# First mixer: the low halves of 38 weight blocks on VectorE instead of GpSimd

## The chip, the cores and the metric

The kernel runs on one core of a Trainium2 chip. The metric is the device time of one execution in microseconds (us); lower is better. A core has engines that run side by side, each through its own list of instructions in order: TensorE (PE in the profile, with the loading of its weights as PEld) multiplies matrices, VectorE (DVE), ScalarE (ACT) and GpSimd (POOL) work element by element, and SyncE (SP) issues most of the loads from HBM.

## The reference

A network of two blocks on 256 tokens of width 1024, in float32. What matters here is the first block's mixer:

```
mod = silu(c) @ w_ada + b_ada                       # 6 x 1024 values: shift, scale, gate, twice
hn  = modulate(rmsnorm(x, norm1_g), shift1, scale1)
qa, ka, va, qi, ki, wi, qb, kb, vb, ga, gb = split(hn @ w_in)
ya  = dsa_attention(...)             # scores by qi, ki, wi choose 64 keys a token; softmax over them
yb  = stick_breaking_attention(qb, kb, vb)
merged = sigmoid(ga) * (ya @ w_proj_a) + sigmoid(gb) * (yb @ w_proj_b)
x   = x + gate1 * (merged @ w_out)
f   = peer_ffn(modulate(rmsnorm(x, norm2_g), shift2, scale2), ...)   # begins with h @ w_q
```

Behind it come the expert layer (`peer_ffn`, whose queries are the "query blocks" below), and the second block with its own mixer, a cross attention and a feed-forward part.

## The kernel before

**Products in two halves.** TensorE gets every operand as a high half (the value rounded to the type of fp32r) and a low half (the value minus the high half), and a product is three matmuls: high by high, high by low and low by high (`mm3`, lines 129 to 131). `weights` (line 90 loads, lines 98 and 100 compute) fetches one block of 128 x 1024 weights, 512 KB, into `wraw`, makes the high half `wh` on ScalarE (L98), and the low half `wl` on VectorE or GpSimd (L100), by the argument `eng`: "v" or "g". There are four buffers for `wraw` and three each for `wh` and `wl`; a `wraw` buffer comes free when both halves are made, a pair of halves when TensorE has read them. A projection block is 24 matmuls on one such weight block. In the lists below a number behind a name tells the buffers of one block from those of another (`wh_1500`, `wl_820`).

**The first mixer.** The first 13 weight blocks (with an order of their own, `ORDER`) end at about 70 us. Then the string `PLAN` sets the order in which steps are written: i and j score the tokens and take the top 64 by eight rounds of max and replace (`index`, L507 to L516, on VectorE), a, v, q and k are projections, s the steps of the first attention (L521 to L645, copies of its transposed weights `pT` at L676, products at L693), 0 to 3 the four pairs of heads of the stick-breaking attention (`stick`: products L708, L731, L745; VectorE at L720 to L739), g one of 16 gate blocks, and r one of 24 adaLN rows. An adaLN row (`ada_one`) is a load of 512 KB and a multiply with a sum over 128 x 1024 elements on VectorE (L266); its two buffers, `lateqx` and `latekx`, are filled in turn. Then the outputs of both attentions are projected (`w_proj`), multiplied by the gates (L568 to L572), split (`mg`, L118 and L119) and projected by `w_out`. The keys and values of the second block's memory are prepared in between (L125, L188, L195, `hm`). At about 290 us the second norm follows (`adaln`, L278 to L281), and the query blocks of the expert layer, the first two of which run together as the norm's columns come.

**What sets the order.** A scheduler of the framework puts each engine's instructions in an order by a model of its own, within the dependences; each engine then goes through its list strictly. Loads of this part are issued in the order of the code (`load`, `in_turn`). So a load that waits for its buffer holds all that follow, and an instruction that waits holds all that stand behind it on its engine.

In the kernel before, the 32 blocks of `w_in` that follow the first 13, the first of each pair of `w_proj` blocks (4), and the first two query blocks have `eng="g"`, 38 in all. 46 blocks of the expert layer, between about 340 and 480 us, have it as well.

Of the kernel before, what the change touches and what calls it, by code (L numbers as in the profile page):

```python
# [31 lines left out]
FIRST = 2  # L32
# [38 lines left out]
class Net:  # L71
# [212 lines left out]
    def first_mixer(self):  # L284
        nc, tc, ap = self.nc, self.tc, self.ap
        with ExitStack() as es:
# [26 lines left out]
            ps = self.ps([128, T], "sm")  # L313
# [25 lines left out]
            hn = self.hi_lo("hn0")  # L339
# [42 lines left out]
            for e in ORDER:  # L382
                if e == "a":
                    k = known
# [20 lines left out]
                with tc.issue_after(norm_exp.ins), tc.issue_after(self.last_rsqrt.ins):  # L405
                    w = self.weights(ap["w_in"][len(first) if e == "w" else 9 + c], next(nlow),
                                     spare.pop() if e == "w" else None)
# [18 lines left out]
            ps = banks[4][:, 0]  # L426
# [10 lines left out]
            def behind():  # L437
                if todo:
                    j = todo.pop(0)
                    self.ada_one(A, j, late[j % 2])  # L440

            def blocks(j0, outs, scale=1.0):
                for j, t in enumerate(outs):
                    ps = self.fm_block(self.weights(ap["w_in"][j0 + j], "g"), hn)
                    yield
                    nc.scalar.activation(t, ps, AF.Copy, scale=scale)  # L446
                    yield

            def chunks(j0, t):
                pss = [self.ps([128, 512], "acc") for _ in range(2)]  # L450
                for k in range(KT):
                    if k % 2 == 0:
                        w = self.weights(ap["w_in"][j0 + k // 2], "g")
                    o = k % 2 * 512
                    for tb in range(2):
                        ts = slice(tb * 128, tb * 128 + 128)
                        self.mm3(pss[tb], (hn[0][:, k, ts], hn[1][:, k, ts]), (w[0][:, o:o + 512], w[1][:, o:o + 512]),
                                 k == 0, k == KT - 1)
                    if k % 2:
                        yield  # L460
                        if k == KT - 1:
                            for tb in range(2):
                                nc.scalar.activation(t[:, tb], pss[tb], AF.Copy)
                        yield

            wi = P.tile([128, 2, 8], FT, name="wi")
            ps = self.ps([128, 2, 8], "sm")
# [4 lines left out]
            with tc.issue_after(qi_last.ins):  # L472
# [4 lines left out]
                ps = self.ps([128, 384], "sm")  # L477
# [8 lines left out]
                for tb in range(2):  # L486
# [3 lines left out]
                                                   ap=[[8 * 384 - 1, 128], [384, 8], [1, n]]))  # L490
# [34 lines left out]
            def attention():  # L525
                pT = None
                for pT in self.probs(P, qa, ka, 8, True, bias, dsa, fine=True):
# [6 lines left out]
            ya, yb = [[P.tile([128, 4, T], FR, name=f"y{c}{i}") for i in range(2)] for c in "ab"]  # L534
            sg = [P.tile([128, 8, T], FT, name=nm) for nm in ("sga", "sgb")]
            gates = blocks(29, [t[:, j] for t in sg for j in range(8)])
            steps = {"i": index(0), "j": index(1), "a": blocks(13, [qa[:, j] for j in range(4)]),
                     "q": blocks(17, [qk[:, 0, j] for j in range(4)], 0.125),
                     "k": blocks(21, [qk[:, 1, j] for j in range(4)]), "v": chunks(25, vb), "s": attention(), "g": gates}
            for hp in range(4):  # L540
                steps[str(hp)] = self.stick(W, hp, qk[:, 0], qk[:, 1], vb, yb)
# [17 lines left out]

            mg = self.hi_lo("mg")  # L560
            for j2 in range(4):
                wa = self.weights(ap["w_proj"][2 * j2], "g")
                wb = self.weights(ap["w_proj"][2 * j2 + 1])
                for i in range(2):
                    j = 2 * j2 + i
                    pa = self.fm_block(wa, ya, 4, i * 512, self.ps([128, T], "acc"))
                    m = W.tile([128, T], FT, name="m")
                    nc.vector.tensor_mul(m, pa, sg[0][:, j])  # L568
                    pb = self.fm_block(wb, yb, 4, i * 512, self.ps([128, T], "acc"))
                    m2 = W.tile([128, T], FT, name="m2")  # L570
                    nc.vector.tensor_mul(m2, pb, sg[1][:, j])
                    nc.vector.tensor_add(m, m, m2)  # L572
                    self.split(mg[0][:, j], mg[1][:, j], m)
                    behind()
# [9 lines left out]
            for j in range(8):  # L584
                ps = self.fm_block(self.weights(ap["w_out"][j]), mg)
# [166 lines left out]
    def peer(self):  # L752
        nc, tc, ap = self.nc, self.tc, self.ap
        hn = self.hn2
        P = self.ctx.enter_context(tc.tile_pool(name="p1", bufs=1))
        with ExitStack() as es:
# [8 lines left out]
            q = carve("q", 16, T)  # L765
            sk = carve("sk", 16, 128)
            nc.scalar.dma_start(sk, ap["sub_keys"])
            ws = [self.weights(ap["peer_wq"][j], "g") for j in range(FIRST)]
            pss = [self.ps([128, T], "acc") for _ in range(FIRST)]
            for k in range(KT):  # L770
                o = slice(k * 128, k * 128 + 128)
# [2 lines left out]
            for j in range(16):  # L774
                ps = pss[j] if j < FIRST else self.fm_block(self.weights(ap["peer_wq"][j]), hn)
# [155 lines left out]
            for e in range(126):  # L931
# [15 lines left out]
                if e >= 96 and e % 2 == 0 and e < 112:  # L947
                    k = (e - 96) // 2
                    nc.vector.tensor_scalar(xg[:, k], x[:, k], g23[:, 0, k:k + 1], None, op0=OP.mult)
                c = v_coef(e)  # L950
                w = self.weights(ap["peer_v"][e])
# [566 lines left out]
```

## Time and profile before

| what | value |
|---|---|
| time, median of 3 runs | 1478.95 us (1477.77 to 1479.18) |
| the profiled execution | 1477.79 us, span of its instructions 1476.0 us |
| mean granted clock of TensorE | 0.982 |
| TensorE busy | 1389.3 us (94% of the span) |
| VectorE busy | 1103.3 us (75%) |
| ScalarE busy | 755.4 us (51%) |
| GpSimd busy | 247.5 us (17%) |
| moved by DMA | 269.52 MB, 183 GB/s in the mean |

The profile is of one execution, so what is read from it stands against 1477.79 us, 1.16 us under the median. Busy shares are means over parts of the program with different limits; TensorE is the fullest engine over the whole, and VectorE in some of its parts. The granted clock is TensorE's share of its full rate: 1.0 is 2.4 GHz, 0.5 is 1.2 GHz. In rows on a wait, what stands behind the arrow is the instruction that ended it.

### The profile page before, as it was taken

The numbers are of one execution on the slowest core, as the hardware profiler recorded it, in microseconds if no ns is written. First come the engines' busy times: TensorE is split into PE (matmuls) and PEld (weight loads), VectorE is DVE, ScalarE is ACT, GpSimd is POOL, SyncE is SP. The second block draws the span as 40 slices with busy tenths as digits, with TensorE's granted clock in tenths as the row PEclk, the third lists the DMA queues.
The fourth block names the chain that finished last, engine by engine and source line by source line (L and its number), as shares of the span: only waits on it lengthen the run. The fifth ranks groups of instructions, "written<-read, shape, count | busy, mean of one in ns | idle before, by whom it ended". The sixth has DMA issues, their size and how long they took to land. (4 is left out here: it accounts for less than half of the span.)

```text
span 1476.0 us, 28894 instructions
## 1 busy us (share of the span) xinstructions
PE 1389.3 (94%) x11584; PEld 1334.0 (90%) x11584; DVE 1103.3 (75%) x2044; ACT 755.4 (51%) x1358; POOL 247.5 (17%) x102
## 2 busy tenths in 40 slices
PE   4987988989998999999999999999999999899997
PEld 3876878989998999999999999999999889789996
DVE  7677868646999988999966555666557786777776
ACT  4544635445445555555454444444445465655555
POOL 3356532105999000000000000000000000000001
PEclk9999989999999999999999999999999999999998
DMA  7765854654555555555566665776564445256562
GB/s 281 250 199 201 280 175 161 205 193 156 174 184 166 173 154 168 158 159 157 165 194 216 202 190 190 228 233 215 186 187 157 128 134 171 72 173 196 189 191 95
DMA packets 76235, 269.52 MB, mean 183 GB/s; under 512 B 8970, under 2 KB 11202, under 8 KB 75460
## 3 DMA queue, kind: packets, MB, share of 16 engines
q1 hardware_dynamic: 71426, 257.99, 54.5%
q10 hardware_dynamic: 4674, 9.69, 1.9%
q8 instruction: 90, 1.47, 0.4%
q14 instruction: 45, 0.37, 0.1%
HBM read 265.01 MB, written 4.21 MB: 182 GB/s over the span
## 5 line engine op out<-in xcount | busy, mean ns | idle before, releaser
L98 ACT ACTIVATE wh<-wraw 128x1024 fp32r<-128x1024 f32 x431 | 456.2, 1060 | 521.1 <-PE ps_acc L130 243.1
L100 DVE TENSOR_TENSOR wl<-wraw,wh 128x1024 fp32r<-128x1024 f32 x346 | 423.9, 1227 | 245.3 <-ACT wh L98 243.9
L129 PE MATMUL ps_acc<-c,wh 128*128 128x256 f32 x1024 | 286.5, 280 | 0.0
L131 PE MATMUL ps_acc<-c,wl 128*128 128x256 f32 x1024 | 286.4, 280 | 0.0
L130 PE MATMUL ps_acc<-c,wh 128*128 128x256 f32 x1024 | 286.4, 280 | 0.0
L100 POOL TENSOR_TENSOR wl<-wraw,wh 128x1024 fp32r<-128x1024 f32 x85 | 228.1, 2700 | 194.0 <-ACT wh L98 151.2
L131 PE MATMUL ps_acc<-hn,wl 128*128 128x256 f32 x696 | 192.7, 277 | 6.2 <-POOL wl L100 6.2
L131 PE MATMUL ps_mm<-hn,wl 128*128 128x256 f32 x680 | 191.3, 282 | 6.4 <-POOL wl L100 6.4
L129 PE MATMUL ps_mm<-hn,wh 128*128 128x256 f32 x680 | 194.7, 286 | 2.0 <-ACT sga L446 1.0
L129 PE MATMUL ps_acc<-hn,wh 128*128 128x256 f32 x696 | 193.9, 279 | 0.0
L129 PEld LDWEIGHTS ps_acc<-c,wh 128*128 128x128 f32 x1024 | 192.5, 188 | 0.1
L130 PE MATMUL ps_acc<-hn,wh 128*128 128x256 f32 x696 | 192.4, 277 | 0.1
L130 PEld LDWEIGHTS ps_acc<-c,wh 128*128 128x128 f32 x1024 | 192.5, 188 | 0.0
L131 PEld LDWEIGHTS ps_acc<-c,wl 128*128 128x128 f32 x1024 | 192.5, 188 | 0.0
L130 PE MATMUL ps_mm<-hn,wh 128*128 128x256 f32 x680 | 191.5, 282 | 0.0
L1404 POOL TENSOR_TENSOR big<-big 128x512 f32<-128x512 f32 x4 | 5.0, 1264 | 982.0 <-DVE big L1401 982.0
L131 PEld LDWEIGHTS ps_mm<-hn,wl 128*128 128x128 f32 x680 | 130.8, 192 | 7.2 <-POOL wl L100 7.2
L131 PEld LDWEIGHTS ps_acc<-hn,wl 128*128 128x128 f32 x696 | 130.7, 188 | 7.2 <-POOL wl L100 7.2
L129 PEld LDWEIGHTS ps_mm<-hn,wh 128*128 128x128 f32 x680 | 131.3, 193 | 4.6 <-issue 1.3
L130 PEld LDWEIGHTS ps_mm<-hn,wh 128*128 128x128 f32 x680 | 131.0, 193 | 0.2
L130 PEld LDWEIGHTS ps_acc<-hn,wh 128*128 128x128 f32 x696 | 130.8, 188 | 0.3 <-DVE hn L281 0.3
L129 PEld LDWEIGHTS ps_acc<-hn,wh 128*128 128x128 f32 x696 | 130.6, 188 | 0.1
(484 smaller groups left out, 2821.9 us busy)
## 6 DMA issues: line engine op xcount, KB each, us to landing
wraw<-in_peer_u_dram SPq DMA_DIRECT2D x128, 512.0 KB, 3.9
wraw<-in_peer_v_dram SPq DMA_DIRECT2D x128, 512.0 KB, 4.2
wraw<-in_w_in_dram SPq DMA_DIRECT2D x70, 512.0 KB, 4.4
wraw<-in_ffn_up_dram SPq DMA_DIRECT2D x44, 512.0 KB, 3.6
wraw<-in_ffn_down_dram SPq DMA_DIRECT2D x22, 512.0 KB, 3.6
ada<-in_w_ada_dram SPq DMA_DIRECT2D x16, 512.0 KB, 6.5
wraw<-in_w_out_dram SPq DMA_DIRECT2D x16, 512.0 KB, 4.5
wraw<-in_peer_wq_dram SPq DMA_DIRECT2D x16, 512.0 KB, 3.6
```

The costliest lines, as they stand in the source:

```text
L98: nc.scalar.activation(h, raw, AF.Copy)
L100: (nc.vector if eng == "v" else nc.gpsimd).tensor_tensor(l, raw, h.bitcast(FT), op=OP.subtract)
L129: mm(out, a[0], b[0], start=first, stop=False, **kw)
L130: mm(out, a[0], b[1], start=False, stop=False, **kw)
L131: self.last_mm = mm(out, a[1], b[0], start=False, stop=last, **kw)
L1404: nc.gpsimd.tensor_tensor(xf[:, tb, cs], xt[:, tb, cs], fg[:, cs], op=OP.mult)
```

## The change

Four calls of `weights` lose their `"g"`, so that the low halves of those 38 blocks are computed by VectorE. The arithmetic is the same.

```
             def blocks(j0, outs, scale=1.0):
                 for j, t in enumerate(outs):
-                    ps = self.fm_block(self.weights(ap["w_in"][j0 + j], "g"), hn)
+                    ps = self.fm_block(self.weights(ap["w_in"][j0 + j]), hn)
...
                     if k % 2 == 0:
-                        w = self.weights(ap["w_in"][j0 + k // 2], "g")
+                        w = self.weights(ap["w_in"][j0 + k // 2])
...
             for j2 in range(4):
-                wa = self.weights(ap["w_proj"][2 * j2], "g")
+                wa = self.weights(ap["w_proj"][2 * j2])
...
-            ws = [self.weights(ap["peer_wq"][j], "g") for j in range(FIRST)]
+            ws = [self.weights(ap["peer_wq"][j]) for j in range(FIRST)]
```

The scheduler also sets other instructions in another order. Three places follow. The first is ScalarE, near the end of the first attention: `wh_1444` and `wh_1500` are high halves of two gate blocks, `sga` and `qk` results of projections, `pT` the transposed weights of the attention's last heads, `ya` its output. Before:

```order
L98 ACTIVATE wh_1444<-wraw_1442 128x1024
L446 ACTIVATE sga_643<-ps_mm_1293 128x256
L98 ACTIVATE wh_1500<-wraw_1498 128x1024
L446 ACTIVATE qk_637<-ps_mm_1328 128x256
L676 ACTIVATE pT0_881<-ps_sm_1354 128x2x128
L676 ACTIVATE pT1_882<-ps_sm_1354 128x2x128
L118 ACTIVATE ya0_639<-ps_sm_1361 128x256
```

and in the changed kernel, on the same engine from the same high half:

```order
L98 ACTIVATE wh_1444<-wraw_1442 128x1024
L446 ACTIVATE qk_637<-ps_mm_1328 128x256
L676 ACTIVATE pT0_881<-ps_sm_1354 128x2x128
L676 ACTIVATE pT1_882<-ps_sm_1354 128x2x128
L1229 DMA mem_1990<-in_mem_dram 128x2048
L118 ACTIVATE ya0_639<-ps_sm_1361 128x256
L118 ACTIVATE ya0_639<-ps_sm_1368 128x256
L98 ACTIVATE wh_1500<-wraw_1498 128x1024
```

The high half `wh_1500` stood ahead of the two copies of `pT`; now it stands behind them and behind two outputs of the attention.

The second place is VectorE ahead of L726 of the third pair of stick-breaking heads (`l1_1704`), on which TensorE's product L731 waits. `junk_1872`, `junk_1875` and `junk_1956` are adaLN rows. Before:

```order
L266 SCALAR_TENSOR_TENSOR junk_1872,mod_82<-lateqx_1121,cond_103 128x1024
L739 TENSOR_TENSOR lb_1484<-lb_1484,upper_98 128x2x2x128
L266 SCALAR_TENSOR_TENSOR junk_1875,mod_82<-latekx_1122,cond_103 128x1024
L270 TENSOR_TENSOR mod_82<-mod_82,b_ada_81 128x8
L582 SCALAR_TENSOR_TENSOR gs_83<-mod_82,vecs_80 128x8
L119 TENSOR_TENSOR yb1_642<-ps_sm_1714,yb0_641 128x256
L720 SCALAR_TENSOR_TENSOR lb_1703<-ps_acc_1696,az_1702 128x384
L720 SCALAR_TENSOR_TENSOR lb_1703<-ps_acc_1699,az_1702 128x384
L721 TENSOR_TENSOR l1_1704<-lb_1703,ps_acc_1696 128x384
L721 TENSOR_TENSOR l1_1704<-lb_1703,ps_acc_1699 128x384
L266 SCALAR_TENSOR_TENSOR junk_1956,mod_82<-lateqx_1121,cond_103 128x1024
L726 TENSOR_TENSOR l1_1704<-l1_1704,upper_98 128x2x2x128
```

and in the changed kernel, the rows that end with the same L726:

```order
L100 TENSOR_TENSOR wl_1784<-wraw_1781,wh_1783 128x1024
L739 TENSOR_TENSOR lb_1484<-lb_1484,upper_98 128x2x2x128
L266 SCALAR_TENSOR_TENSOR junk_1824,mod_82<-lateqx_1121,cond_103 128x1024
L270 TENSOR_TENSOR mod_82<-mod_82,b_ada_81 128x8
L266 SCALAR_TENSOR_TENSOR junk_1827,mod_82<-latekx_1122,cond_103 128x1024
L119 TENSOR_TENSOR yb1_642<-ps_sm_1714,yb0_641 128x256
L720 SCALAR_TENSOR_TENSOR lb_1703<-ps_acc_1696,az_1702 128x384
L720 SCALAR_TENSOR_TENSOR lb_1703<-ps_acc_1699,az_1702 128x384
L721 TENSOR_TENSOR l1_1704<-lb_1703,ps_acc_1696 128x384
L721 TENSOR_TENSOR l1_1704<-lb_1703,ps_acc_1699 128x384
L100 TENSOR_TENSOR wl_1832<-wraw_1829,wh_1831 128x1024
L726 TENSOR_TENSOR l1_1704<-l1_1704,upper_98 128x2x2x128
```

The rows 1872, 1875 and 1956 have moved behind L726, and low halves have come in among the others.

The third place is VectorE at the end of the first top-k (`acc0`, L515) and the beginning of the second (`acc1`). `wl_820`, `wl_852`, `wl_924` and `wl_942` are low halves of the projections a, a, v and q. Before:

```order
L507 SCALAR_TENSOR_TENSOR acc1_635<-rel_696,wi_613,acc1_635 128x256
L514 MATCH_REPLACE acc0_634<-m8_667,acc0_634 128x128
L515 TENSOR_SCALAR acc0_634<-acc0_634 128x128
L516 TENSOR_TENSOR acc0_634<-acc0_634,cm_94 128x128
L507 SCALAR_TENSOR_TENSOR acc1_635<-rel_706,wi_613,acc1_635 128x256 x2
L507 SCALAR_TENSOR_TENSOR acc1_635<-rel_710,wi_613,acc1_635 128x256 x2
L513 MAX m8_714<-acc1_635 128x8
L514 MATCH_REPLACE acc1_635<-m8_714,acc1_635 128x256
```

and in the changed kernel:

```order
L507 SCALAR_TENSOR_TENSOR acc1_635<-rel_696,wi_613,acc1_635 128x256
L515 TENSOR_SCALAR acc0_634<-acc0_634 128x128
L100 TENSOR_TENSOR wl_820<-wraw_817,wh_819 128x1024
L516 TENSOR_TENSOR acc0_634<-acc0_634,cm_94 128x128
L507 SCALAR_TENSOR_TENSOR acc1_635<-rel_706,wi_613,acc1_635 128x256 x2
L507 SCALAR_TENSOR_TENSOR acc1_635<-rel_710,wi_613,acc1_635 128x256 x2
L100 TENSOR_TENSOR wl_852<-wraw_849,wh_851 128x1024
L513 MAX m8_714<-acc1_635 128x8
L100 TENSOR_TENSOR wl_924<-wraw_921,wh_923 128x1024
L514 MATCH_REPLACE acc1_635<-m8_714,acc1_635 128x256
L100 TENSOR_TENSOR wl_942<-wraw_939,wh_941 128x1024
```

Four low halves stand among the rounds of the top-k now.

## Rows read from the trace of the kernel before

**Rows 1.** Busy time of the engines by stretch, in us, with granted clock and DMA.

```profile
core 0: us, PE busy (x) PEld busy (x) DVE busy (x) ACT busy (x) POOL busy (x), PEclk, DMA share, GB/s
66.00:113.00 47.00, 42.07 (x286) 36.71 (x285) 31.23 (x88) 23.02 (x47) 26.08 (x11) 0.96 0.60 193
113.00:196.00 83.00, 64.94 (x509) 57.91 (x509) 71.64 (x98) 44.27 (x93) 44.89 (x18) 0.93 0.67 238
196.00:256.00 60.00, 54.15 (x404) 52.04 (x403) 40.81 (x72) 29.34 (x45) 17.16 (x7) 0.90 0.49 164
...
66.00:300.00 234.00, 203.31 (x1550) 188.11 (x1549) 174.77 (x310) 117.31 (x218) 92.88 (x37) 0.94 0.60 202
```

**Rows 2.** TensorE's waits, 66 to 300 us: total us, times, longest.

```profile
PE ps_sm L693 <- ACT pT L676: 7.0, 1, 7.0
PE ps_sm L731 <- DVE l L726: 5.3, 1, 5.3
PE ps_mm L131 <- POOL wl L100: 3.8, 2, 2.2
PE ps_acc L131 <- POOL wl L100: 2.9, 2, 1.5
...
PE ps_acc L131 <- DVE wl L100: 2.7, 2, 2.4
PE ps_sm L188 <- DVE yb L119: 1.8, 1, 1.8
```

**Rows 3.** Groups, 66 to 300 us: busy us, mean ns; idle before, its releasers.

```profile
L100 POOL TENSOR_TENSOR wl<-wraw,wh 128x1024 fp32r<-128x1024 f32 x37 | 92.9, 2521 | 137.6 <-ACT wh L98 95.0 <-DVE diag L218 41.6 <-PE ps_sm L469 1.1
...
L100 DVE TENSOR_TENSOR wl<-wraw,wh 128x1024 fp32r<-128x1024 f32 x17 | 20.8, 1222 | 2.6 <-ACT wh L98 1.7
```

**Rows 4.** Groups of VectorE, 113 to 196 us.

```profile
L266 DVE SCALAR_TENSOR_TENSOR junk<-lateqx,cond 128x1024 f32<-128x1024 f32 x9 | 17.8, 1982 | 0.8 <-DMA lateqx<-in_w_ada_dram 0.8
L266 DVE SCALAR_TENSOR_TENSOR junk<-latekx,cond 128x1024 f32<-128x1024 f32 x8 | 16.5, 2064 | 1.0 <-DMA latekx<-in_w_ada_dram 1.0
L645 DVE TENSOR_SCALAR bias<-bias,st 128x256 f32<-128x256 f32 x8 | 6.2, 816 | 0.0
...
L739 DVE TENSOR_TENSOR lb<-lb,upper 128x512 f32<-128x512 f32 x2 | 3.6, 1776 | 0.9 <-ACT lb L738 0.9
L635 DVE TENSOR_SCALAR st<-st 128x2 f32<-128x2 f32 x4 | 2.8, 701 | 0.0
```

**Rows 5.** Line 266, the whole span: ns shortest/median/longest.

```profile
L266 DVE SCALAR_TENSOR_TENSOR junk<-lateqx,cond x12: 1207/1225/3422, 126.8 to 234.3; 128x1024 f32<-128x1024 f32 x12
```

**Rows 6.** Timeline, 129 to 148 us: start, us, instruction, idle before.

```profile
129.71 11.09 POOL L100 TENSOR_TENSOR wl<-wraw,wh 128x1024 fp32r<-128x1024 f32 x4 [3.42 <-ACT wh L98]
...
135.17 3.42 DVE L266 SCALAR_TENSOR_TENSOR junk<-lateqx,cond 128x1024 f32<-128x1024 f32 x1
...
139.05 0.86 SPq L90 DMA_DIRECT2D wraw<-in_w_in_dram  x2
...
144.87 1.06 ACT L98 ACTIVATE wh<-wraw 128x1024 fp32r<-128x1024 f32 x1 [7.75 <-DMA wraw<-in_w_in_dram]
...
147.06 0.42 DVE L119 TENSOR_TENSOR ya<-ps_sm,ya 128x256 fp32r<-128x256 f32 x1 [3.61 <-ACT ya L118]
```

**Rows 7.** Timeline of VectorE, 120 to 123 us.

```profile
120.27 0.15 DVE L635 TENSOR_SCALAR st<-st 128x2 f32<-128x2 f32 x1
...
122.27 0.60 DVE L645 TENSOR_SCALAR bias<-bias,st 128x256 f32<-128x256 f32 x2
```

**Rows 8.** Timeline of VectorE, 189 to 194 us.

```profile
189.92 2.74 DVE L266 SCALAR_TENSOR_TENSOR junk<-lateqx,cond 128x1024 f32<-128x1024 f32 x1
...
192.59 0.68 DVE L726 TENSOR_TENSOR l<-l,upper 128x512 f32<-128x512 f32 x1
```

**Rows 9.** Timeline of VectorE, 234 to 238 us.

```profile
234.27 3.42 DVE L266 SCALAR_TENSOR_TENSOR junk<-lateqx,cond 128x1024 f32<-128x1024 f32 x1
```

**Rows 10.** Timeline of TensorE and VectorE, 82 to 84 us.

```profile
82.58 0.28 PE L129 MATMUL ps_mm<-hn,wh 128*128 128x256 f32 x1
...
83.54 0.23 DVE L515 TENSOR_SCALAR acc<-acc 128x128 f32<-128x128 f32 x1
```

## The prediction, made before the changed kernel ran

> **What bounds the kernel now.** I read five views, from wide to narrow. The first is the busy time of each engine by stretch [rows 1]. All but one of the moved subtractions run between 66 and 300 us, 37 of the 38 (the other stands just ahead of it). In these 234.0 us TensorE works 203.3 us and stands 30.7 us, and the granted clock is 0.94, which means it spent part of the stretch at 1.2 GHz instead of 2.4. Everything that the change can win lies in these two numbers; a reader should see that the rest of the span can only shift. The second view is TensorE's waits in that stretch [rows 2]. The six rows carry 23.5 of the 30.7 us. Only 6.7 us (3.8 and 2.9) name the moved operation itself. The two longest single waits, 7.0 us for a copy on ScalarE and 5.3 us for a VectorE multiply, don't name it, and the question is whether they hang on it all the same.
>
> The third view, the groups by line [rows 3], says that they do. One low half takes 2.52 us on GpSimd and 1.22 us on VectorE. But VectorE pays for GpSimd's work too: the adaLN rows of L266 take between 1.21 and 3.42 us [rows 5], and their mean in the stretch 113 to 196, by their two buffers, is 1.98 and 2.06 us [rows 4]. The long ones lie beside GpSimd: while four subtractions run there one behind the other from 129.7 to 140.8, a row of L266 takes 3.42 us [rows 6]. So an operation with two operands in SBUF stands on VectorE until GpSimd has finished its own. The stretch 113 to 196 is the tight one: VectorE is busy 71.6 of 83.0 us, more than TensorE's 64.9 [rows 1].
>
> **The change, stage by stage.** It removes 38 operations of about 2.5 us from GpSimd and adds 38 of 1.22 us to VectorE, 46 us in all. Nothing is added to ScalarE or the load queue. The order of the instructions changes on VectorE, ScalarE and (from 230 us on) TensorE.
>
> *113 to 196 us: 18 operations.* VectorE's work first. Added: 18 x 1.22 = 22.0 us. Given back: the 17 rows of L266 take 17.8 + 16.5 = 34.3 us and would take 17 x 1.21 = 20.6, so 13.7; L645 takes 6.2 us for eight that take 0.60 a pair undisturbed, so 3.8; L739 takes 3.6 for two, where the same shape takes 0.68 in L726, so 2.2; L635 takes 2.8 for four of 0.15, so 2.2 [rows 4, 5, 7, 8]. Together 21.9 us. VectorE's work stays as it is: 71.6 - 21.9 + 22.0 = 71.7 us. What changes is when its results come.
>
> The 7.0 us wait: TensorE stands at 139.8 for the copy of pT, and that copy stands on ScalarE behind the high half wh_1500, which waits 7.75 us for its weights to land [rows 6]. Their load was issued at 139.05, since the queue's load before it refills the buffer of the stretched L266 row, which ended at 138.5. In the new order wh_1500 stands behind both pT copies, and the row of L266 isn't stretched. This wait goes. What is late next is the load itself, which the block two further on needs. The 5.3 us wait for L726: in the old order three rows of L266 (1872, 1875 and 1956) stand ahead of it, the last of them 2.74 us long [rows 8]; in the new one all three stand behind it, and one low half (wl_1832) comes ahead. This wait goes too, unless VectorE as a whole is late.
>
> So the stage is bounded by VectorE from both sides. If its 11.4 us of idle time (83.0 - 71.6) stay, nothing is won. If all of it goes and the three deferred rows (3 x 1.21 = 3.6 us) fall into later idle time as well, 15 us are won; TensorE's 64.9 us would allow 18. I take 7: 3.6 us of VectorE's idle time lie inside the 7.0 us wait (it waits 3.61 us for ScalarE, until 147.1 [rows 6]), and 3.6 are the deferred rows.
>
> *196 to 256 us: 7 operations.* VectorE is busy 40.8 of 60.0 us and has room [rows 1]. The waits here are 1.4 us of the 2.9 for GpSimd, 2.4 us of the 2.7 for a low half that already is on VectorE, and 1.8 us for yb [rows 2]. The 2.4 us one stands behind an L266 row of 3.42 us [rows 9], stretched by GpSimd, and goes with it. Yb stands behind an L266 row as well, and goes. Of the 1.4 us I let half stay, since the low half stands on VectorE behind a product of the same block (L568). That is 0.7 + 2.4 + 1.8 = 4.9, taken as 5. The clock is 0.90 here, so 60 x 0.10 = 6.0 us of work at most are lost to it; how much comes back with fewer waits no row tells. I leave it out of the sum and let it widen the range below.
>
> *66 to 113 us: 11 operations.* Given back: 3.8 us of waits for GpSimd's low halves [rows 2], and of the clock's loss at most 47 x 0.04 = 1.9 us [rows 1]. Charged: the new order sets wl_820 behind L515, the end of the first top-k, at 83.8 [rows 10]; with 1.22 us it is there at 85.0. The block that wants it began at 82.6 [rows 10] and wants it with its third product, at 82.8: 2.2 us. The next one (wl_852) stands behind four accumulations more and costs about 1 us by the same count. A third (wl_992) stands behind most of the second top-k, which is interleaved with the softmax of the first half: 22 operations of 0.1 to 0.7 us, some 10 us, while TensorE has three blocks of 2.9 us to do: some 2.5 us late, counting the head start of a microsecond. Charged 5.7, given back 3.8 to 5.7. I take zero, with 3 us on either side.
>
> *256 to 300 us: 2 operations (query blocks).* Given back at most the other 1.5 us of the 2.9 [rows 2]. Charged: both low halves now stand on VectorE ahead of the adaLN products L278, 2 x 1.22 = 2.4 us at most, against which VectorE's rows there are no longer stretched. Zero, between 1.5 won and 2.4 lost.
>
> Sum: 7 + 5 + 0 + 0 = 12 us. The profiled execution took 1477.8 us (span 1476.0), 1.2 us under the median of the runs; 1477.8 - 12 = 1465.8, and as a median **1467 us**.
>
> **Rivals.**
> *VectorE's work decides, and nothing comes of it.* In the tight stage its work stays at 71.7 us; if its idle time is a matter of waiting for landings and for ScalarE, the two long waits come back under other names, and the 5 us of the later stage are eaten by the 5.7 us of the first. Time: 1479, within 3 us. For it: the sum of work; the loads of L266 and of weights share one queue in a fixed order, and the DMA share is 0.67 in this stage already. Against it: both long waits lose the instruction that stands in front of them. The Trainium skill (Perfetto Trace Analysis, Optimizing Scalar/DVE Operations) says that VectorE and GpSimd share a read port, so that moving work between the two might not help, and that a full VectorE may be relieved by giving work to GpSimd, the opposite of this change; by that rule no change or worse would come, and the trace agrees as far as the sum of work goes.
>
> *Slower: VectorE stands at the head of its queue.* A low half waits for its high half. On GpSimd that waiting cost nobody: 95.0 us in 37 operations, 2.6 us each; the 17 low halves that VectorE had in the same stretch waited 2.6 us in all, 0.15 each [rows 3]. On VectorE everything behind it waits too: softmax, stick-breaking, and the rows whose end lets the next load go. Over 18 operations that is between 2.7 and 47 us. The gains of 15 (the upper bound of the stage) and 5 us are used up at 20/18 = 1.1 us each; at 1.5 us each the kernel takes 27 - 20 = 7 us longer, 1486. For it: the high halves come late whenever a buffer of three is still read by TensorE. Against it: the 0.15 us, measured in a stretch where ScalarE made the halves for both engines.
>
> *Everything goes.* All waits of [rows 2] in the two middle stages and most of the clock's loss: 15 + 5.6 + 6 + 2 = 29 us, 1450. Against it: VectorE's 71.7 us.
>
> **How the numbers follow.** Forecast (5 to 24 us won) 0.66; nothing comes 0.15; slower by the queue 0.14; everything goes 0.05. Under 0.2%, 3 us, a measurement of this kernel can't tell a change from none. Faster: 0.66 + 0.05 + 0.04 from the edge of the second case = 0.75; same 0.11; slower 0.14. The forecast's own range is 1455 to 1474; with the second case it reaches to 1480, and some 0.05 below and 0.12 above are left out.
>
> **What would show it.** Right: L266 at 1.2 us in all its rows between 113 and 250; no TensorE wait of over 3 us for pT or for L726; the third L726, at 192.6 in [rows 8], some 7 us earlier, with VectorE's work up to there unchanged; the wait for a low half behind the row of [rows 9] gone. Wrong: new waits of TensorE for VectorE's low halves that sum to over 10 us between 66 and 256, or VectorE idle behind high halves by over 1 us each, or the two long waits back at the same places with another releaser. My first-stage charges are right if TensorE waits near the end of each top-k for a low half.

## The result: 27 us faster, more than double the forecast

| kernel | median, us | runs | ratio to before, 95% interval |
|---|---|---|---|
| before | 1479.07 (1477.77 to 1480.18) | 4 | |
| changed | 1451.71 (1450.79 to 1455.18) | 4 | 0.9821 [0.9806, 0.9836] |
| changed, measured again beside other kernels | 1449.90 (1448.48 to 1450.74) | 5 | 0.9803 [0.9775, 0.9830] |

The forecast was 1467 us, from 1455 to 1480. The direction was right and the size was not: 27.4 us were won where 12 were forecast, and the time came out near the rival that had 0.05, "everything goes" (1450).

The first comparison is by stage. The places are the same instructions in both traces, so that the stages hold the same work of TensorE: the start of L469, of the attention products L609 (113.7 us before, 111.2 after), of L731 of the third pair, of the first `w_out` product and of the first L800 of the expert layer. Before, and then after (columns as in [rows 1]):

```profile
69.92:113.72 43.80, 38.87 (x269) 34.19 (x269) 31.23 (x88) 20.39 (x43) 24.41 (x11) 0.96 0.59 192
113.72:193.42 79.70, 61.64 (x498) 55.65 (x497) 69.06 (x92) 44.27 (x93) 44.17 (x17) 0.94 0.68 241
193.42:255.61 62.19, 56.34 (x404) 53.32 (x405) 43.00 (x78) 29.00 (x44) 17.16 (x7) 0.88 0.48 162
255.61:307.79 52.18, 47.22 (x398) 46.29 (x397) 34.08 (x58) 25.42 (x42) 5.04 (x3) 1.00 0.61 198
```

```profile
68.72:111.23 42.51, 37.60 (x269) 32.55 (x268) 36.59 (x99) 20.66 (x43) 0.00 (x0) 1.00 0.62 199
111.23:178.30 67.07, 60.52 (x497) 54.77 (x497) 56.85 (x102) 43.39 (x91) 0.00 (x0) 1.00 0.70 251
178.30:229.07 50.77, 49.85 (x409) 47.39 (x407) 45.80 (x90) 30.65 (x47) 0.00 (x0) 1.00 0.71 238
229.07:280.62 51.55, 48.14 (x395) 46.58 (x395) 34.52 (x61) 24.69 (x42) 0.29 (x1) 1.00 0.64 206
```

A stage's gain is split into TensorE's idle time (span minus PE busy) and its busy time, which for the same matmuls differs by the granted clock:

| stage | gain, us | of it idle time | of it busy time | forecast |
|---|---|---|---|---|
| first | 1.29 | 4.93 - 4.91 = 0.02 | 1.27 | 0 |
| second (the tight one) | 12.63 | 18.06 - 6.55 = 11.51 | 1.12 | 7 |
| third | 11.42 | 5.85 - 0.92 = 4.93 | 6.49 | 5 |
| fourth | 0.63 | 4.96 - 3.41 = 1.55 | -0.92 | 0 |

Idle time gives 18.0 us and busy time 8.0, and 1.2 us were won ahead of the first place. The split between idle and busy time is that of these two executions; a second one of the changed kernel, between the same places, is as short with 20.6 us from idle time (237.87 - 204.08 = 33.8 before) and 5.1 from busy time:

```profile
sum 212.11, PE 198.94 PEld 184.37 DVE 173.89 ACT 119.76 POOL 0.29; mean PE 66.31 PEld 61.46 DVE 57.96 ACT 39.92 POOL 0.10
```

The waits that answer to [rows 2], TensorE from 66 to 275 us of the changed kernel:

```profile
PE ps_mm L131 <- DVE wl L100: 7.5, 8, 2.1
PE ps_mm L129 <- ACT wh L98: 2.6, 2, 2.0
PE ps_sm L731 <- DVE l L726: 0.8, 1, 0.8
PE ps_sm L731 <- DVE yb L119: 0.7, 1, 0.7
PE ps_sm L668 <- ACT pT L676: 0.6, 1, 0.6
```

The 7.0 us wait for pT is gone, and the 5.3 us one is 0.8. VectorE's groups in the tight stage (111 to 180 us), which answer to [rows 4]:

```profile
L100 DVE TENSOR_TENSOR wl<-wraw,wh 128x1024 fp32r<-128x1024 f32 x15 | 18.2, 1222 | 5.9 <-ACT wh L98 5.0 <-PE ps_acc L609 1.0
L266 DVE SCALAR_TENSOR_TENSOR junk<-lateqx,cond 128x1024 f32<-128x1024 f32 x8 | 9.8, 1221 | 0.2
L266 DVE SCALAR_TENSOR_TENSOR junk<-latekx,cond 128x1024 f32<-128x1024 f32 x7 | 8.5, 1219 | 4.5 <-DMA latekx<-in_w_ada_dram 4.5
...
L645 DVE TENSOR_SCALAR bias<-bias,st 128x256 f32<-128x256 f32 x8 | 2.4, 350 | 0.0
...
L739 DVE TENSOR_TENSOR lb<-lb,upper 128x512 f32<-128x512 f32 x2 | 1.4, 689 | 0.8 <-ACT lb L738 0.8
...
L635 DVE TENSOR_SCALAR st<-st 128x2 f32<-128x2 f32 x4 | 0.7, 162 | 0.0
```

Each of the 24 late rows of L266 takes 1.21 to 1.23 us now. In the line that answers to [rows 5] the longest is 1226 ns:

```profile
L266 DVE SCALAR_TENSOR_TENSOR junk<-lateqx,cond x12: 1216/1219/1226, 123.9 to 219.8; 128x1024 f32<-128x1024 f32 x12
```

### The profile page after: what moved, and what is told of

The parts are those of the page before. It is cut to its first block, busy times and chain, and to the rows that moved or that the text cites. A ratio compares the mean times of both kernels' runs of the same rounds, so it can differ in the third digit from the quotient of the medians.

```text
span 1449.8 us, 28871 instructions
## 1 busy us (share of the span) xinstructions
PE 1382.8 (95%) x11584; PEld 1326.8 (92%) x11584; DVE 1102.9 (76%) x2082; ACT 756.3 (52%) x1358; POOL 151.3 (10%) x64
## 5 line engine op out<-in xcount | busy, mean ns | idle before, releaser
L100 DVE TENSOR_TENSOR wl<-wraw,wh 128x1024 fp32r<-128x1024 f32 x384 | 470.3, 1227 | 253.9 <-ACT wh L98 251.1
L129 PE MATMUL ps_mm<-hn,wh 128*128 128x256 f32 x680 | 192.6, 283 | 2.7 <-ACT wh L98 2.6
L130 PE MATMUL ps_mm<-hn,wh 128*128 128x256 f32 x680 | 189.5, 279 | 0.0
L100 POOL TENSOR_TENSOR wl<-wraw,wh 128x1024 fp32r<-128x1024 f32 x47 | 131.8, 2826 | 56.4 <-ACT wh L98 56.2
L129 PEld LDWEIGHTS ps_mm<-hn,wh 128*128 128x128 f32 x680 | 128.9, 190 | 5.2 <-ACT wh L98 3.3
L130 PEld LDWEIGHTS ps_mm<-hn,wh 128*128 128x128 f32 x680 | 128.5, 189 | 0.2
```

The costliest lines, as they stand in the source:

```text
L100: (nc.vector if eng == "v" else nc.gpsimd).tensor_tensor(l, raw, h.bitcast(FT), op=OP.subtract)
L129: mm(out, a[0], b[0], start=first, stop=False, **kw)
L130: mm(out, a[0], b[1], start=False, stop=False, **kw)
```

## The experiments

Two theories were to be told apart. By the first, the gain is VectorE's stretching: an operation of GpSimd holds VectorE up, and without it the same operations are short. By the second, it is order: what stands in front of pT and of L726. Beside the times I give the stretched time on VectorE from 66 to 300 us, counted for each shape as the time over its shortest tenth of rows (where it is over 0.1 us). By this count it is 37.3 us in the kernel before and 0 in the changed one. The count is a lower bound, since it misses a shape whose every row is long, as the single rows of L515 and L582; measured against the durations of the changed kernel, the stretching before is 41.4 us. Edits below are shortened to the lines that matter.

**GpSimd's subtractions back, everything else as in the changed kernel.** The lists of the other engines hold what they hold in the changed kernel, in the same order.

```
+        return (nc.gpsimd.tensor_tensor(self.extra, raw[:, :896], h.bitcast(FT)[:, :896], op=OP.subtract) if eng == "d" else 0) and (h, l) or (h, l)
...
+                    ps = self.fm_block(self.weights(ap["w_in"][j0 + j], "d"), hn)
```

> The changed kernel, in which GpSimd also computes 36 of the low halves (the first 896 of their 1024 columns; those of w_in and w_proj) into a buffer that nobody reads. VectorE's low halves are the ones used. Every engine but GpSimd has exactly the order of the changed kernel. If what the change won came from VectorE no longer being stretched by GpSimd, most of the 27 us are lost again: 1465 to 1480 us, with L266 rows of up to 3.4 us back and about 30 us more of VectorE's busy time between 66 and 280. If it came from the order of instructions (wh_1500 behind pT, the adaLN rows behind L726) and from the lower cost on one's own queue, it stays within 4 us of 1452.

Measured: 1501.04 us, ratio 1.0156 [1.0110, 1.0201]; 52.3 us stretched. GpSimd, then two groups of VectorE, 66 to 330 and 66 to 300 us:

```profile
L101 POOL TENSOR_TENSOR extra<-wraw,wh 128x896 f32<-128x896 f32 x35 | 89.8, 2567 | 107.4 <-ACT wh L98 97.7 <-DMA wraw<-in_w_in_dram 4.3 <-issue 3.5
```

```profile
L100 DVE TENSOR_TENSOR wl<-wraw,wh 128x1024 fp32r<-128x1024 f32 x51 | 87.5, 1721 | 6.5 <-ACT wh L98 4.6 <-PE ps_acc L609 1.0
L266 DVE SCALAR_TENSOR_TENSOR junk<-latekx,cond 128x1024 f32<-128x1024 f32 x12 | 18.9, 1577 | 0.9 <-DMA latekx<-in_w_ada_dram 0.9
```

Work whose result nobody reads costs 49 us. The low halves themselves go from 1.22 to 1.72 us. It is 21 us more than the kernel before in the same comparison (1480.51), since VectorE now has both the 38 low halves and the stretching. It came out 21 us above the range that I gave the first theory, and the second is excluded as the main cause.

Another way in which the subtractions could cost time is that GpSimd holds the buffers of `wraw` and `wh` longer. The trace puts little down to it: the loads waited 1.9 us for GpSimd in all (66 to 300 us), and ScalarE's high halves 1.0.

```profile
SPq L90 <- POOL extra L101: 1.9, 1, 1.9
```

The tight stage, between the same two places as above, isn't shorter for the changed order while the stretching stands:

```profile
126.01:208.69 82.68, 66.14 (x497) 59.20 (x497) 77.50 (x99) 43.61 (x90) 38.17 (x15) 0.90 0.57 202
```

With the order of the changed kernel, and its low halves on VectorE, it lasts 82.7 us, 3.0 more than before, and VectorE is busy 77.5 us of them.

**A copy on GpSimd instead**, one operand read from SBUF; same order.

```
+        return (nc.gpsimd.tensor_copy(self.extra, raw[:, :896]) if eng == "d" else 0) and (h, l) or (h, l)
```

> The same, but what GpSimd does beside is a copy of the block (896 of 1024 columns): one operand read from SBUF instead of two. The order of the other engines is that of the changed kernel. If VectorE is stretched only by GpSimd's operations with two operands, this stays within 4 us of 1452 with L266 at 1.2 us; if any work of GpSimd on SBUF stretches it, or if the weight buffers that GpSimd holds longer cost the time, it goes to 1462 or more like the kernel with the subtraction.

Measured: 1461.01 us, 0.9884 [0.9843, 0.9925]; 8.1 us stretched. GpSimd's group:

```profile
L101 POOL COPY extra<-wraw 128x896 f32<-128x896 f32 x35 | 42.2, 1205 | 118.2 <-DMA wraw<-in_w_in_dram 90.5 <-DMA wraw<-in_w_proj_dram 27.4
```

Neither expectation holds: a copy stretches as well, but less (L266 at most 1.95 us), and 9 us are lost. A GpSimd operation half as long (1.2 against 2.6 us) costs a sixth of the stretching. That the 9 us are near the 8.1 is no rule: from the first L469 to the first L800, TensorE's idle time is 219.56 - 204.12 = 15.4 us here and 211.90 - 196.10 = 15.8 in the changed kernel, and its busy time for the same matmuls is 8.0 us more.

```profile
sum 219.56, PE 204.12 PEld 189.55 DVE 181.32 ACT 120.52 POOL 38.78; mean PE 68.04 PEld 63.18 DVE 60.44 ACT 40.17 POOL 12.93
```

So in this execution the loss stands in the granted clock (0.95 to 0.97, against 1.00) and not in longer waits in sum; how the copies bring that about stays open.

**Order alone**, with the low halves on GpSimd: high halves behind pT, adaLN rows behind L726.

```
+        with self.tc.issue_after(self.last_pt.ins) if ...: nc.scalar.activation(h, raw, AF.Copy)
+        with self.tc.issue_after(self.last_l1.ins) if ...: self.last_ada = nc.vector.scalar_tensor_tensor(junk, ...)
```

> The kernel before, with its low halves on GpSimd, in which two orders alone are changed: the high halves of this stage stand behind the copies of pT that precede them in the program, and the adaLN rows behind the L726 that precedes them. If the waits of 7.0 and 5.3 us are a matter of what stands ahead of pT and of L726, 7 to 12 us are won: 1467 to 1472. If VectorE's stretching decides, the waits come back under other names and it stays within 4 us of 1479.

Measured: 1503.80 us, 1.0166 [1.0129, 1.0202]. Both expectations are wrong, and the experiment was too coarse. The edit holds every adaLN row of the stage, and with it the loads. TensorE's first wait, and loads on SyncE between 145 and 181 us:

```profile
PE ps_mm L129 <- ACT wh L98: 27.7, 5, 12.0
```

```profile
145.22 2.66 SPq L90 DMA_DIRECT2D wraw<-in_w_in_dram  x2
171.89 0.33 SPq L90 DMA_DIRECT2D latekx<-in_w_ada_dram  x1
...
180.82 0.42 SPq L90 DMA_DIRECT2D wraw<-in_w_in_dram  x1
```

No load of weights is issued for 33 us (147.9 to 180.8), because the load ahead of them waits for a row that has been put off. So this run says nothing of the 7.0 us wait. The next one says something of it.

**One high half moved**: wh_1500 alone behind pT.

```
+        with self.tc.issue_after(self.last_pt.ins) if src is self.ap.get("late") else ExitStack(): nc.scalar.activation(h, raw, AF.Copy)
-  self.weights(ap["w_in"][j0 + j], "g")
+  self.weights(ap.setdefault("late", ap["w_in"][j0 + j]) if j0 + j == 32 else ap["w_in"][j0 + j], "g")
```

> The kernel before with one constraint: the high half of one gate block, wh_1500, stands behind the copies of pT on ScalarE, as in the changed kernel; low halves stay on GpSimd. If the 7.0 us wait hangs on that place in ScalarE's list alone, 4 to 7 us are won: 1473 to 1476. If VectorE's stretching makes the whole stage late, the wait comes back within the next blocks, for a high half or a low half, and the time stays within 3 us of 1479.

Measured: 1479.66 us, 1.0001 [0.9980, 1.0021]; 39.5 us stretched. TensorE's longest wait, and ScalarE and VectorE ahead of its end:

```profile
PE ps_sm L693 <- DVE ya L119: 6.1, 1, 6.1
```

```profile
137.63 3.26 DVE L266 SCALAR_TENSOR_TENSOR junk<-latekx,cond 128x1024 f32<-128x1024 f32 x1
...
143.78 1.06 ACT L98 ACTIVATE wh<-wraw 128x1024 fp32r<-128x1024 f32 x1 [5.08 <-DMA wraw<-in_w_in_dram]
...
146.35 1.98 DVE L266 SCALAR_TENSOR_TENSOR junk<-latekx,cond 128x1024 f32<-128x1024 f32 x1 [4.03 <-DMA latekx<-in_w_ada_dram]
...
148.26 0.74 DVE L119 TENSOR_TENSOR ya<-ps_sm,ya 128x256 fp32r<-128x256 f32 x2
```

The wait of 7.0 us goes and comes back as one of 6.1 at the same line L693, now for VectorE's `ya`. This `ya` stands behind a row of L266 that waited 4.03 us for its load, and the buffer of that load had been held until 140.9 by a row stretched to 3.26 us. So moving this high half behind pT changes the time by no more than the interval, some 3 us either way. The order isn't wholly that of the changed kernel: here wh_1500 (at 143.78) still stands ahead of ScalarE's `ya`, and there it stands behind. The full order was run only together with the low halves on VectorE, in the runs above.

**Parts of the change.** Gates only (`"gv"[j0 == 29]`); a, v, q and k only (`"vg"[j0 == 29]`, `chunks` without `"g"`); `w_proj` and query blocks only.

> Of the change only the 16 gate blocks' low halves go to VectorE; the other 22 stay on GpSimd. Most of the gate blocks lie in the stretch 113 to 196 us of the kernel before. If that stretch gives about 14 of the 27 us, as the landmarks of the two traces say, this wins 10 to 16 us: 1463 to 1469. If the gain needs GpSimd to be empty, because each remaining low half stretches VectorE as before, under 6 us.

> Of the change only the 16 low halves of the projections a, v, q and k go to VectorE; gates, w_proj and query blocks stay on GpSimd. The gates alone won 17.6 us of the 27.4. If the gain is the stretching given back, place by place, this part and the w_proj part share the other 10 us: 4 to 8 us here, 1471 to 1475. If the parts need each other (one GpSimd queue that must be empty), under 3 us.

> Of the change only the six low halves of w_proj and of the first query blocks go to VectorE. By places: the waits of 1.4 and 2.4 us for low halves of w_proj go, so 2 to 5 us: 1474 to 1477. If nothing is won where the gates' subtractions ahead of it have made VectorE late already, 1479.

| part | median, us | ratio, 95% interval | stretched, us: 66 to 300 / 113 to 196 |
|---|---|---|---|
| before | 1479.12 | | 37.3 / 24.0 |
| 16 gates | 1461.87 | 0.9874 [0.9835, 0.9912] | 17.5 / 5.4 |
| 16 of a, v, q, k | 1474.84 | 0.9969 [0.9949, 0.9990] | 25.9 / 16.2 |
| 6 of w_proj and query blocks | 1472.32 | 0.9954 [0.9936, 0.9971] | 30.5 / 25.6 |
| all 38 | 1449.90 | 0.9803 [0.9775, 0.9830] | 0 / 0 |

The ratio of the gates belongs to another series, in which the kernel before took 1480.51 us; the other rows were measured beside 1479.12. The windows of the last column are of time, so a faster kernel has other work in them. The shares, 1.26 + 0.31 + 0.46 = 2.03%, are the 1.97% of the whole, within their intervals. The parts don't need each other. The gates carry most, with 16 of 38 operations. Between the same two places as above, the tight stage lasts 70.4 us with the gates moved, 74.4 with a, v, q and k, and 80.0 with the third part, against 79.7 before: the gates take most of the stretching out of it. The gates and the third part came out 1.1 and 1.7 us under the ranges that I gave them, the second near the slow end of its range.

**A made wait**: ten unused subtractions on VectorE ahead of one low half of `w_proj`.

```
+        more = [nc.vector.tensor_tensor(self.extra, raw[:, :896], h.bitcast(FT)[:, :896], op=OP.subtract) for _ in range(10 * (eng == "x"))]; ...
```

> The changed kernel, in which ten subtractions that nobody uses stand on VectorE ahead of one low half of w_proj (second pair), about 10 us, in a stretch where TensorE never waits. It shows what a wait of TensorE costs beside its own length. If the granted clock falls to 0.5 behind such a wait, the end moves by the waits' length plus half of the low stretch (a stretch of 3.4 us at 0.5 would be 1.7 us). If the clock has other causes, it stays 1.0 from 35 to 280 us and the end moves by the waits' length alone.

Measured in one execution: 1462.96 us, 11.3 more than the changed kernel. The first window goes from the start of TensorE's first wait to the end of its last, and two of 4.16 us follow:

```profile
214.36:226.84 12.48, 1.06 (x4) 0.61 (x4) 12.38 (x16) 0.79 (x1) 0.00 (x0) 0.62 0.00 0
226.84:231.00 4.16, 4.16 (x19) 4.16 (x20) 3.32 (x5) 0.42 (x1) 0.00 (x0) 0.50 0.76 251
231.00:235.16 4.16, 4.16 (x37) 4.16 (x36) 3.80 (x8) 1.50 (x3) 0.00 (x0) 1.00 0.78 284
```

TensorE stands 11.4 us; then 19 matmuls go at 1.2 GHz where 37 go at 2.4 GHz. That is 2 us more beside the wait. The first L800, at 280.62 us in the changed kernel, comes at 293.21, 12.6 us later, where the wait and the 2 us together would be 13.5. So the clock fell in this wait and rose again behind it; only one such wait was made, and the time is of one run.

**GpSimd relieved further**, by the four low halves of the first 13 blocks (`LOWS` all "v"), and by the 46 of the expert layer (`u_block(e, 0, "v")`).

> The changed kernel with the four low halves of the first 13 weight blocks that GpSimd still makes moved to VectorE too. In 0 to 66 us VectorE is busy 51.7 us, of which about 9 us are stretching. If giving back the stretching pays here as well, 1 to 4 us are won: 1448 to 1451. If VectorE's added 4 x 1.2 us stand in front of the adaLN rows that set the pace there, it is 1 to 4 us slower.

> The changed kernel again, beside the next one: 1450 to 1455 us by its first four runs.

> The changed kernel with the four low halves of the first 13 weight blocks on VectorE too, again, in more rounds beside the changed kernel. Its trace reaches the same wait for a low half near 80 us 2.9 us earlier. If that is carried to the end: 1448 to 1450, 2 to 4 us under the changed kernel; if a later stage takes it back: within 1.5 us of it.

Measured, the four: 1449.41 us, 0.9790 [0.9751, 0.9828]; again 1448.35, 0.9789 [0.9761, 0.9817], beside the changed kernel's 1449.90 (0.1 under the range that I gave it). The intervals overlap almost wholly; whether the 1.5 us are there stays open.

> The changed kernel with the 46 low halves of the expert layer's first blocks (320 to 480 us) moved to VectorE too, so that GpSimd makes none but four of them. VectorE is busy 157.1 of 160 us there. 46 x 1.22 = 56 us are added. If little is given back there (8 rows of a 2048-wide operation at 4.4 us and others look stretched, about 30 us by the shape next to them), it is 25 to 56 us slower: 1477 to 1508. If relief from GpSimd pays everywhere, it is faster than 1452.

Measured, the 46: 1516.31 us in two runs, 1.0255 [1.0209, 1.0300], 65 us more than the changed kernel and 8 above the range. TensorE's waits there (300 to 480 us), the engines from 339 to 394 us, and two groups of VectorE, first of the changed kernel and then of this one:

```profile
PE ps_sm L849 <- DVE big L831: 36.5, 2, 30.0
PE ps_mm L131 <- DVE wl L100: 27.8, 2, 17.1
```

```profile
339.00:394.00 55.00, 5.52 (x24) 4.94 (x25) 54.97 (x213) 0.00 (x0) 0.00 (x0) 0.50 0.06 18
```

```profile
L826 DVE TENSOR_TENSOR big<-io,big 128x2048 f32<-128x2048 f32 x4 | 17.7, 4422 | 0.0
...
L808 DVE CAST big<-big 128x256 f32<-128x256 uint32 x2 | 5.0, 2494 | 0.0
```

```profile
L826 DVE TENSOR_TENSOR big<-io,big 128x2048 f32<-128x2048 f32 x4 | 9.1, 2278 | 0.0
...
L808 DVE CAST big<-big 128x256 f32<-128x256 uint32 x2 | 0.6, 279 | 0.0
```

The stretching goes here as well, from 4.4 to 2.3 us. But in the changed kernel VectorE is full there (157 of 160 us), 56 us are added, and the low halves stand in one list with the top-k of the experts: TensorE waits 64 us, where it waits 8.9 in the changed kernel. It isn't the slower rival of the prediction, in which VectorE stands behind high halves: in the stretch shown VectorE works without a break, and TensorE stands behind it. It is a place where VectorE has no room.

## Why the prediction was wrong, step by step

- **The tight stage, first failed step: "VectorE's work stays as it is: 71.6 - 21.9 + 22.0 = 71.7".** VectorE's busy time fell from 69.06 to 56.85 us, 12.2. Its idle time stayed: 79.70 - 69.06 = 10.6 before, 67.07 - 56.85 = 10.2 after. So the stage became shorter by what VectorE's work in it became shorter, which agrees with VectorE bounding it, as the prediction held. This is argued from the sums and not exact: in the other runs VectorE's idle time in the stage lies between 5.2 us (subtractions back) and 13.1 (a, v, q and k). The sum by groups shows why the work didn't stay: 18.2 us of low halves were added, 15 of them and not 18 (17 subtractions lay between the two places before, and the others fall just outside now); L266 gave 16.0, not 13.7, since two of its rows left the stage too; and L522 (1.8) and L582 (2.3) were stretched and weren't in my list. L645, L739 and L635 gave 3.8, 2.2 and 2.1, as counted from [rows 4, 7, 8]. These groups make 10.0 of the 12.2 us; most of the rest is overlap of neighbouring rows, which the busy time counts once. So about 4 us are stretching that I had overlooked, and about 6 are work that now stands outside the stage.
- **The same stage, the 7 us taken.** Half of them was to come out of VectorE's idle time by the new order, and half from three L266 rows put off. The idle time hardly changed, so the first half didn't come in this way; of the rows two left the stage, 2.4 us and not 3.6. Both waits went, as forecast, and no run shows that the order alone takes them away: with the same order and the stretching back the stage lasts 82.7 us, and wh_1500 moved alone changes nothing clear of noise. The trace of that run shows stretched rows holding buffers, and so loads, and so the instructions behind them. What the deferral of the L266 rows alone gives stays open, since the run for it held up the loads.
- **Second failed step: the clock left out of the sum.** I bounded it at 6.0 and 1.9 us and counted zero. The busy time of the same matmuls fell by 6.49 and 1.27 us in these stages, and by 1.12 in the tight one. The value lay near the bounds. The granted clock is 1.0 from 35 to 281 us in this execution; in a second one of the same kernel it fell for 3.4 us at three places before 281. There the busy time fell by 204.08 - 198.94 = 5.1 us, and the four stages are as short all the same. So this term is worth 5 to 8 us, and part of what the clock takes came out of time in which TensorE would have waited.
- **196 to 256 us, waits.** Forecast 4.9, measured 4.93; that they agree so closely is partly luck, since two executions of one kernel differ by more. The wait behind the row of [rows 9] went, and so did the one of L188 for yb; a wait of 0.7 for yb stands at L731 now.
- **66 to 113 us.** Waits for low halves stand at the ends of the top-k: 1.13 and 1.08 us near 82 and 87 us, 1.51 at 101.5. I charged 2.2, 1 and 2.5. Together 3.7 against 3.8 given back: zero, as forecast.
- **Rival "nothing comes".** Its premise, that VectorE's work decides, agrees with the sums above, and its arithmetic (mine, 71.7) was wrong. The Trainium skill (Perfetto Trace Analysis, Optimizing Scalar/DVE Operations) says that moving work between the two might not help; here it gave 27 us. The stretched time given back, 37.3 us by the count and 41.4 against free durations, nearly pays for the 46 us added (VectorE's busy time over the four stages is 177.36 us before and 173.75 after), and 24 us of it lay in the tight stage.
- **Rival "slower by the head of the queue".** VectorE stood 9.1 us behind high halves for 54 low halves, 0.17 each, where 1.1 was the point from which it decides.
- **Rival "everything goes".** Its terms, 15 and 5.6 us of waits and 6 and 2 us of clock, measured 11.5, 4.9, 6.5 and 1.3. What I held against it was VectorE's 71.7 us, the wrong sum.
- **Signs.** L266 at 1.2 us, no wait over 3 us and the third L726 earlier all came; it starts at 175.83 us instead of 192.59, 16.8 earlier and not 7, and VectorE's work up to there was not unchanged.

So the failed steps are two terms: VectorE's work in the tight stage (0 instead of 12.2 us less) and the clock (0 instead of 5 to 8).

## What to carry to other kernels

When an engine bounds a stage, look at the spread of each shape's duration before counting its work: what is long beside another engine's operation is not its own work, and it comes back when that engine falls silent. A wait named at one instruction may be lateness of the whole engine; moving that instruction alone may then only rename the wait, as it did here. And give the clock a term of its own in the sum, with a range: the same matmuls took 5.1 and 8.0 us less in two executions of the changed kernel.

## What was not expected of the hardware

Which operations GpSimd stretches shows in means from 66 to 300 us, before and then after:

```profile
L515 DVE TENSOR_SCALAR acc<-acc 128x256 f32<-128x256 f32 x1 | 2.5, 2485 | 0.0
...
L572 DVE TENSOR_TENSOR m<-m,m 128x256 f32<-128x256 f32 x8 | 4.9, 616 | 0.0
L568 DVE TENSOR_TENSOR m<-ps_acc,sga 128x256 f32<-128x256 f32 x8 | 3.4, 419 | 2.6 <-PE ps_acc L131 2.5
```

```profile
L515 DVE TENSOR_SCALAR acc<-acc 128x256 f32<-128x256 f32 x1 | 0.3, 284 | 0.0
...
L572 DVE TENSOR_TENSOR m<-m,m 128x256 f32<-128x256 f32 x8 | 3.4, 419 | 0.0
L568 DVE TENSOR_TENSOR m<-ps_acc,sga 128x256 f32<-128x256 f32 x8 | 3.4, 420 | 0.5 <-PE ps_acc L131 0.4
```

The rule that I drew from the trace named operations with two operands in SBUF only, though my sum already had L645 and L635 in it, which are scalar operations. Those with two are stretched (L572), and those with one operand in PSUM aren't (L568); but a scalar operation with one SBUF operand is (L515, 2485 against 284 ns), and so is a cast (L808 above). The top-k's MAX8 isn't (424 and 419 ns for 256 columns), nor the reduction L634 (664 and 673). The Trainium skill (SBUF — State Buffer, Who interferes with whom) says just this: two SBUF inputs contend with a GpSimd operation that reads SBUF, copies, casts and scalar operations can, a reduction doesn't. The traces agree in each of the shapes named here; a stretched copy on VectorE is not among them.

Where every row of a shape is stretched, its shortest row hides it: L826 was long in all four rows, and only the run without GpSimd there showed its 2.28 us.
